# Sliding windows of an image batch: the last two units swapped, and the unit (14, 0) stored by GpSimd's indirect scatter in place of eight plain stores on SyncE's queue

## The chip, the cores and the metric

The kernel runs on one core of a Trainium2 chip. The metric is the device time of one execution in microseconds (us). The time of before is a median of 3 runs, and beside it stands one execution that the hardware profiler recorded. All times of single instructions come from that one execution.

## The reference: what is computed

The input `x` has 16 images of 64 channels, 64 rows and 64 columns in float32 (16.8 MB). The output holds every 8x8 window at a stride of 4. There are 15 window positions down (i) and 15 across (j), so 3600 windows of 64x8x8 elements, 59 MB. Nothing is calculated; bytes are copied from one layout to another.

```python
def reference(x, window_size, stride):
    n_h = (h - window_size) // stride + 1      # 15
    n_w = (w - window_size) // stride + 1      # 15
    result = np.zeros((batch, n_h, n_w, c, window_size, window_size), dtype=np.float32)
    for i in range(n_h):
        for j in range(n_w):
            result[:, i, j] = x[:, :, i*stride:i*stride+window_size, j*stride:j*stride+window_size]
    return result
```

One window of one image, `out[b, i, j]`, is 16 KB (64 channels x 64 floats x 4 bytes) and lies in one piece in device memory. "A row" below means these 16 KB.

## The kernel before, in words

**Input.** The whole input sits in one SBUF tile `L` (line 49). A partition holds 32 channels and 16 image rows of one image: partition number = 64 x channel half + 4 x image + image quarter (a quarter is 16 of the 64 rows). Loads (lines 103 to 107) go out on two queues: SyncE's (SP) takes 28 of the 32 channels of the first channel half, GpSimd's (POOL) the other four and all of the second half.

**Index tiles.** GpSimd makes a row of partition numbers (line 68), VectorE (DVE) computes from it the number of the output row that each partition writes (lines 79 to 101): `idx` for all rows, `idx_y0` and `idx_y1` for the images 0 to 7 or 8 to 15 alone, `idx_hi` and `idx_lo` for the lowest windows, where one of the 16 positions doesn't exist. A partition that has nothing to write gets an index beyond the bounds, and the scatter drops it.

**Units.** The output is made in units `(j, s)`: j is the window column, s is 0 or 2. A unit is one `G` tile of 128 partitions x 16 KB (line 112): one half of the partitions takes the windows that begin at slot s of each quarter (4 rows to a slot), the other half those of slot s + 1. There are four `G` tiles, used in turn. `fill` (lines 130 to 142) copies the windows out of `L`. For s = 0 ScalarE (ACT) does one copy of 64 partitions and DVE the other, for each half (line 172). For s = 2 (lines 182 to 184) ACT does both copies of slot 2, and DVE makes slot 3 with two copies and two shuffles, since slot 3 takes its lower four rows from the neighbouring partition. Which half takes slot 3 alternates with j (`turn`). Slot 3 of the last quarter doesn't exist, so such a unit writes 64 rows of slot 2 and 48 of slot 3, 112 rows; a unit with s = 0 writes 128.

**Stores.** `scatter` (lines 118 to 128) issues one indirect DMA on GpSimd's queue, which writes up to 128 rows of 16 KB. The stores are declared free of one another (lines 114 to 116), so no store waits for another one. A fill waits until the store that last read its `G` tile has landed, four units earlier.

**Order.** Six units over half of the images come first (lines 148 to 161), then the list `units` (line 164): for each j the unit (j, 0), if it wasn't among the first ones, and then (j, 2). Line 165 takes the second to last unit out of the list and puts it at its end, so that the last units are (13, 0), (13, 2), (14, 2), (14, 0). All units but the last go out by `scatter`. The last, (14, 0), goes out by eight plain DMAs on SP's queue (lines 176 to 179), one for each image quarter and slot, each of 16 rows, 256 KB. SP issues nothing else between the loads and these eight.

Of the kernel before, what the change touches and what calls it, by code (L numbers as in the profile page):

```python
# [10 lines left out]
def kernel(  # L11
# [7 lines left out]
    nc = tc.nc  # L19
# [11 lines left out]
    CH = 2  # L31
    HQ = P // (B * CH)
    CL = C // CH
    RB = H // HQ
    NSLOT = RB // ST
# [25 lines left out]
    def itile(name):  # L61
        return ipool.tile([P, 1], i32, name=name)

    pi, tb, tq, tc_, th, idx, idx_y0, idx_y1, idx_lo, idx_hi = (
        itile(n) for n in ("pi", "tb", "tq", "tc", "th", "idx", "idx_y0", "idx_y1", "idx_lo", "idx_hi")
    )
# [44 lines left out]
    NG = 4  # L111
    G = [gpool.tile([P, C, WS, WS], f32, name=f"G{n}") for n in range(NG)]

    def free(st):
        tc.declare_no_dep(st.ins, group="stores", reason="each store writes rows of its own")
        tc.add_to_no_dep_group("stores", st.ins)

    def scatter(g, ix, j, s):
        st = nc.gpsimd.indirect_dma_start(  # L119
            out=o_v,  # L120
            out_offset=bass.IndirectOffsetOnAxis(ap=ix[:, 0:1], axis=0),
            in_=g.rearrange("p c r w -> p (c r w)"),
            in_offset=None,
            element_offset=(s * NW + j) * CFREE,
            bounds_check=B * NWIN - 1,
            oob_is_err=False,
        )
        free(st)

    def fill(g, half, s, j, lo, n, copies):  # L130

        d = slice(half * HP + lo, half * HP + lo + n)
        cols = slice(j * ST, j * ST + WS)
        for ch in (half, 1 - half):
            f = slice(ch * HP + lo, ch * HP + lo + n)
            cs = slice(ch * CL, (ch + 1) * CL)
            copy = copies[ch != half]
            if s < NSLOT - 1:
                copy(out=g[d, cs, :, :], in_=L[f, :, s * ST : s * ST + WS, cols])  # L139
            else:  # L140
                copy(out=g[d, cs, 0:ST, :], in_=L[f, :, s * ST : RB, cols])  # L141
                nc.vector.stream_shuffle(out=g[d, cs, ST:WS, :], in_=L[f, :, 0:ST, cols], mask=nxt)  # L142
# [12 lines left out]
    for y in range(NY):  # L155
        for j in range(EARLY):
            for half in range(CH):
                copies = (dve, dve) if y and half and j == 1 else (act, dve)
                fill(G[t % NG], half, half, j, y * QP, QP, copies)
            scatter(G[t % NG], (idx_y0, idx_y1)[y], j, 0)  # L160
            t += 1


    units = [(j, s) for j in range(NW) for s in (0, 2) if s or j >= EARLY]
    units.append(units.pop(-2))
    o_q = out.rearrange("b i j c r w -> i j b (c r w)")
    for j, s in units:
        g = G[t % NG]
        t += 1
        if s == 0:  # L170
            for half in range(CH):
                fill(g, half, s + half, j, 0, HP, (act, dve))
            if (j, s) != units[-1]:
                scatter(g, idx, j, s)
                continue
            g_q = g.rearrange("(ch b q) c r w -> ch q b (c r w)", ch=CH, q=HQ)
            for q in range(HQ):
                for half in range(CH):
                    free(nc.sync.dma_start(out=o_q[q * NSLOT + s + half, j], in_=g_q[half, q]))
        else:  # L180

            turn = j % 2
            fill(g, turn, s, j, 0, HP, (act, act))
            fill(g, 1 - turn, s + 1, j, 0, HP, (dve, dve))
            scatter(g, (idx_hi, idx_lo)[turn], j, s)
# [35 lines left out]
```

## Time and profile before

| what | value |
|---|---|
| median of 3 runs (lowest to highest) | 196.81 us (196.72 to 196.84) |
| the profiled execution's own time | 196.84 us |
| its span, first to last instruction | 195.1 us |
| time of that execution outside the span | 1.74 us |
| DVE busy | 132.0 us (68%) |
| ACT busy | 123.6 us (63%) |
| POOL busy | 51.8 us (27%) |
| DMA, mean over the span | 75.81 MB at 389 GB/s |
| of it by GpSimd's queue (q0) | 66.34 MB, 83.3% of the span of 16 DMA engines |
| of it by SP's queue (q1) | 9.44 MB, 13.5% |
| indirect stores | 32, of 957 to 2194 ns on POOL; 5.9 to 20.5 us to landing |
| plain stores on SP | 8, 539 to 2418 ns each on SP's queue, from 175.0 us on |

Read it in this way. A busy share is a mean over stages that differ. DMA here means the 16 DMA engines that both queues share. "To landing" is the time from the issue of a DMA until its semaphore says that all bytes are written.

### The profile page before, as it was taken

The numbers are of one execution on the slowest core, as the hardware profiler recorded it, in microseconds if no ns is written. First come the engines' busy times: TensorE is split into PE (matmuls) and PEld (weight loads), VectorE is DVE, ScalarE is ACT, GpSimd is POOL, SyncE is SP. The second block draws the span as 40 slices with busy tenths as digits, with TensorE's granted clock in tenths as the row PEclk, the third lists the DMA queues.
The fourth block names the chain that finished last, engine by engine and source line by source line (L and its number), as shares of the span: only waits on it lengthen the run. The fifth ranks groups of instructions, "written<-read, shape, count | busy, mean of one in ns | idle before, by whom it ended". The sixth has DMA issues, their size and how long they took to land.

```text
span 195.1 us, 485 instructions
## 1 busy us (share of the span) xinstructions
DVE 132.0 (68%) x156; ACT 123.6 (63%) x66; POOL 51.8 (27%) x53
## 2 busy tenths in 40 slices
DVE  6877778895999998766577657774776667750000
ACT  0000008961999999999779677977797779752000
POOL 7402211107462134123313113231323132210000
DMA  2999999999999999999999999999999999999983
GB/s 87 316 403 403 398 402 394 403 399 408 420 375 380 386 420 403 427 420 415 430 430 415 417 417 420 423 423 420 430 423 420 420 427 410 410 418 420 329 259 124
DMA packets 11588, 75.81 MB, mean 389 GB/s; under 512 B 3888, under 2 KB 3888, under 8 KB 7984
## 3 DMA queue, kind: packets, MB, share of 16 engines
q0 software_dynamic: 9472, 66.34, 83.3%
q1 hardware_dynamic: 2112, 9.44, 13.5%
q14 instruction: 4, 0.03, 0.0%
HBM read 16.78 MB, written 69.21 MB: 441 GB/s over the span
## 4 chain that ended last, share of the span: by engine, by line
DMA 66%; DVE 17%; issue 3%; POOL 2%; ACTq 1%; ACT 1%; DVEq 0%; PEldq 0%
DMA out_dram<-G,idx 21%; DMA L<-in_x_dram 18%; DMA out_dram<-G,idx_hi 15%; DMA out_dram<-G,idx_lo 12%; DVE G L139 8%; DVE G L142 6%; DVE G L141 2%; POOL L L57 2%; ACTq L216 1%; ACT G L139 1%; DVEq L139 0%; POOL pi L68 0%; DVEq L141 0%; PEldq L216 0%; ACTq L139 0%
## 5 line engine op out<-in xcount | busy, mean ns | idle before, releaser
L139 ACT COPY G<-L 64x2048 f32<-64x2048 f32 (+1 forms) x65 | 122.3, 1896 | 23.5 <-DMA out_dram<-G,idx 9.9
L139 DVE COPY G<-L 64x2048 f32<-64x2048 f32 (+1 forms) x37 | 44.8, 1221 | 16.7 <-DMA out_dram<-G,idx 11.4
L142 DVE STREAM_SHUFFLE G<-L 64x1024 f32<-64x1024 f32 x30 | 38.3, 1276 | 0.0
L141 DVE COPY G<-L 64x1024 f32<-64x1024 f32 x30 | 20.7, 691 | 18.5 <-DMA out_dram<-G,idx_hi 10.4
L153 DVE MEMSET G<- 32x4096 f32 x8 | 27.8, 3472 | 7.9 <-issue 6.2
L139 ACT ACT_TABLE_LOAD x1 | 1.3, 1283 | 29.8 <-DMA L<-in_x_dram 29.8
L119 POOL DMA_INDIRECT out_dram<-G,idx_hi x8 | 11.7, 1461 | 30.3 <-DVE G L142 17.9
L119 POOL DMA_INDIRECT out_dram<-G,idx x11 | 11.4, 1040 | 30.6 <-ACT G L139 30.6
L57 POOL DMA_DIRECT2D L<-in_x_dram x16 | 9.8, 626 | 25.2 <-DMA L<-in_x_dram 24.7
L119 POOL DMA_INDIRECT out_dram<-G,idx_lo x7 | 9.1, 1304 | 20.5 <-ACT G L139 14.3
L119 POOL DMA_INDIRECT out_dram<-G,idx_y x6 | 9.4, 1559 | 13.4 <-DVE G L139 8.5
L77 DVE TENSOR_TENSOR th<-tc,tq 128x1 int32<-128x1 int32 x2 | 0.3, 160 | 0.1
L77 DVE CUSTOM_DVE_ANT_0 idx_y<-idx,th 128x2 uint16<-128x2 uint16 x2 | 0.3, 158 | 0.1
L74 DVE TENSOR_SCALAR th<-tc 128x1 int32<-128x1 int32 x2 | 0.3, 154 | 0.1
L68 POOL IOTA pi<- 128x1 int32 x1 | 0.1, 125 | 0.4 <-PEq L216 0.4
L77 DVE CUSTOM_DVE_ANT_0 idx_hi<-idx,th 128x2 uint16<-128x2 uint16 x1 | 0.2, 160 | 0.0
L142 DVE LOAD_MASK_SELECT G<-L x30 | 0.2, 6 | 0.0
L77 DVE CUSTOM_DVE_ANT_0 idx_lo<-tb,th 128x2 uint16<-128x2 uint16 x1 | 0.2, 159 | 0.0
L77 DVE CUSTOM_DVE_ANT_0 idx_lo<-idx_lo,th 128x2 uint16<-128x2 uint16 x1 | 0.2, 159 | 0.0
L77 DVE CUSTOM_DVE_ANT_0 idx<-tb,th 128x2 uint16<-128x2 uint16 x1 | 0.2, 159 | 0.0
L77 DVE CUSTOM_DVE_ANT_0 tb<-tb,th 128x2 uint16<-128x2 uint16 x1 | 0.2, 158 | 0.0
L91 DVE TENSOR_SCALAR th<-th 128x1 int32<-128x1 int32 x1 | 0.2, 153 | 0.0
(13 smaller groups left out, 1.7 us busy)
## 6 DMA issues: line engine op xcount, KB each, us to landing
L<-in_x_dram POOLq DMA_DIRECT2D x8, 1024.0 KB, 21.2
L<-in_x_dram SPq DMA_DIRECT2D x8, 896.0 KB
out_dram<-G SPq DMA_DIRECT2D x8, 256.0 KB
L<-in_x_dram POOLq DMA_DIRECT2D x8, 128.0 KB, 21.3
out_dram<-G,idx POOLq DMA_INDIRECT x11, 14.6
out_dram<-G,idx_hi POOLq DMA_INDIRECT x8, 13.9
out_dram<-G,idx_lo POOLq DMA_INDIRECT x7, 14.1
out_dram<-G,idx_y POOLq DMA_INDIRECT x6, 6.3
```

Of the source, the lines that this page charges most:

```text
L57: eng.dma_start(out=L[p0 : p0 + QP - HQ + 1 : HQ, c0:c1, :, :], in_=x_v[ch, y, q, :, c0:c1, :])
L68: nc.gpsimd.iota(pi[:, :], pattern=[[0, 1]], base=0, channel_multiplier=1)
L74: nc.vector.tensor_scalar(out=d[:, :], in0=a[:, :], scalar1=float(m), scalar2=None, op0=ALU.mult)
L77: nc.vector.tensor_tensor(out=d[:, :], in0=a[:, :], in1=b[:, :], op=op)
L91: nc.vector.tensor_scalar(out=th[:, :], in0=th[:, :], scalar1=-1.0, scalar2=FAR, op0=ALU.mult, op1=ALU.add)
L119: st = nc.gpsimd.indirect_dma_start(out=o_v, out_offset=bass.IndirectOffsetOnAxis(ap=ix[:, 0:1], axis=0), in_=g.rearrange("p c r w -> p (c ...
L139: copy(out=g[d, cs, :, :], in_=L[f, :, s * ST : s * ST + WS, cols])
L141: copy(out=g[d, cs, 0:ST, :], in_=L[f, :, s * ST : RB, cols])
L142: nc.vector.stream_shuffle(out=g[d, cs, ST:WS, :], in_=L[f, :, 0:ST, cols], mask=nxt)
L153: nc.vector.memset(G[t][p0 : p0 + QP, :, :, :], 0.0)
L216: with _tile.TileContext(nc) as tc:
```

## The change

Line 165 goes, so the last two units stand in the order (14, 0), (14, 2). The branch for the last unit goes too: (14, 0) is stored by `scatter` with `idx` like every other unit with s = 0, and (14, 2), now the last, by `scatter` with `idx_hi` as before. SP issues no stores any more. `free` is written out where it was called; that alters no instruction. Lines 67 to 107, which make the index tiles and issue the loads, and line 158, which hands copies to ACT or DVE, are the same in both kernels.

```diff
-    def free(st):
-        tc.declare_no_dep(st.ins, group="stores", reason="each store writes rows of its own")
-        tc.add_to_no_dep_group("stores", st.ins)
...
-        free(st)
+        tc.declare_no_dep(st.ins, group="stores", reason="each store writes rows of its own")
+        tc.add_to_no_dep_group("stores", st.ins)
...
     units = [(j, s) for j in range(NW) for s in (0, 2) if s or j >= EARLY]
-    units.append(units.pop(-2))
-    o_q = out.rearrange("b i j c r w -> i j b (c r w)")
     for j, s in units:
         g = G[t % NG]
         t += 1
         if s == 0:
             for half in range(CH):
                 fill(g, half, s + half, j, 0, HP, (act, dve))
-            if (j, s) != units[-1]:
-                scatter(g, idx, j, s)
-                continue
-            g_q = g.rearrange("(ch b q) c r w -> ch q b (c r w)", ch=CH, q=HQ)
-            for q in range(HQ):
-                for half in range(CH):
-                    free(nc.sync.dma_start(out=o_q[q * NSLOT + s + half, j], in_=g_q[half, q]))
+            scatter(g, idx, j, s)
         else:
             turn = j % 2
             fill(g, turn, s, j, 0, HP, (act, act))
             fill(g, 1 - turn, s + 1, j, 0, HP, (dve, dve))
             scatter(g, (idx_hi, idx_lo)[turn], j, s)
```

## The prediction

> **What bounds the kernel now.** I read the page's slices first, then the chain, then the tail in stretches, and then who ends last. The slices are 4.9 us wide; the first row is the share of the 16 DMA engines that is busy, the second what they move.
>
> ```profile
> DMA  2999999999999999999999999999999999999983
> GB/s 87 316 403 403 398 402 394 403 399 408 420 375 380 386 420 403 427 420 415 430 430 415 417 417 420 423 423 420 430 423 420 420 427 410 410 418 420 329 259 124
> ```
>
> From the third slice to the 37th the engines move some 400 to 430 GB/s: transfers bound the kernel. Then, in the last three slices, the rate falls to 329, 259 and 124. This is all that the change can touch, since the instructions ahead of the last two units are the same. The chain of work that ended last, from 140 us on, says what comes before that:
>
> ```profile
> 143.35 14.34 DMA out_dram<-G,idx
> 157.68 15.29 DMA out_dram<-G,idx_hi
> 172.98 0.02 issue
> ...
> 173.06 1.90 ACT G L139
> 174.96 1.92 ACTq L216
> ```
>
> The last fill begins when the store (12, 2) has landed, at 172.98, and frees its tile. From there the chain is cut off, so I looked at the tail by stretches of 2 us (stretch, DVE, ACT, POOL, clock, DMA share, GB/s).
>
> ```profile
> 172.00:174.00 2.00, 0.93 (x1) 0.94 (x1) 0.46 (x1) 1.00 1.06 442
> ...
> 182.00:184.00 2.00, 0.00 (x0) 0.00 (x0) 0.00 (x0) 1.00 0.99 336
> ...
> 186.00:188.00 2.00, 0.00 (x0) 0.00 (x0) 0.00 (x0) 1.00 0.80 246
> 188.00:190.00 2.00, 0.00 (x0) 0.00 (x0) 0.00 (x0) 1.00 0.79 262
> 190.00:192.00 2.00, 0.00 (x0) 0.00 (x0) 0.00 (x0) 1.00 0.84 238
> ```
>
> No engine computes after 177, yet the rate drops. The timeline and the rows of the last line that SP and POOL run (L216, the end of the program) name the two things that are late:
>
> ```profile
> 171.50 0.96 POOL L119 DMA_INDIRECT out_dram<-G,idx_hi  x1 [3.79 <-ACT G L139]
> 173.06 3.82 ACT L139 COPY G<-L 64x2048 f32<-64x2048 f32 x2 [2.35 <-DMA out_dram<-G,idx_hi]
> 173.07 2.48 DVE L139 COPY G<-L 64x2048 f32<-64x2048 f32 x2 [2.34 <-DMA out_dram<-G,idx_hi]
> 174.98 14.82 SPq L179 DMA_DIRECT2D out_dram<-G  x8
> ```
>
> ```profile
> L216 SPq EVENT_SEMAPHORE  x11: 17/28/28, 192.0 to 195.0; - x11
> L216 POOLq DRAIN  x3: 51/105/22757, 171.3 to 194.8; - x3
> ```
>
> First: SP needs 14.82 us to issue eight stores of 256 KB, until 189.8. Eight times 256 KB in 14.8 us is 142 GB/s, a third of what the engines can take, so once GpSimd's queue runs dry the engines starve. Second: POOL's first drain begins at 171.3 and takes 22.76 us, to 194.04. By the semaphore records of the trace the last scatter landed at 192.02 (issue 171.50 plus the longest time to landing, 20.5) and the last SP store at 194.14. SP's wait for it ends at 194.16, its own drain at 194.29, and the span ends 0.8 us later with the closing barrier.
>
> **The change part by part.** Sums are against the profiled execution: span 195.1, own time 196.84, so 1.74 us lie outside the span. The median of the runs shown is 196.81, so the two can be used as one.
>
> *Removed: eight plain stores.* 14.82 us on SP's queue go. Nothing was behind them but the end. What goes with them is the starved tail.
>
> *Moved: (14, 0) ahead of (14, 2).* The fill of (14, 0) takes the slot of (14, 2), at 166.88. ACT's two copies are the same (3.82 us, to 170.7), DVE's are shorter (2.48 against 3.83). So its scatter is issued at 171.5, where that of (14, 2) is now. The scatter adds one DMA_INDIRECT on POOL (0.96 to 1.78 us in the timeline after 60 us). POOL has its gap of 2 to 4 us before each scatter, so this costs nothing; the scatter behind it waits for copies until 177.7. Then (14, 2) is filled from 173.06, when (12, 2) has landed: ACT 3.82 us, DVE 3.83, both to 176.9. POOL starts 0.8 us later (170.7 to 171.50 in the row above), at 177.7, and is through by 179.5.
>
> *Is that early enough?* The price of a late scatter is a hole in the transfers. The first scatter of the kernel, issued at 44.53, has its first packets of over 8 KB in the stretch 46 to 48, so a scatter takes at most 3.5 us to its first rows: 181.2 at the latest here. By the semaphore records, the 16 increments of a scatter come in two bunches of eight: half of the engines run ahead. (13, 0) landed at 174.2 on the early half, at 176.8 on the late half, and on one engine at 177.6. A row of 16 KB takes 0.627 us on one engine (418 GB/s from 60 to 170 us, over 16). The early half has 16 rows to do for (13, 2) and (14, 0), so it is busy to 174.2 + 10.0 = 184.2. That leaves 3 us, so no hole.
>
> *When the last row lands.* Each engine has 22 rows left after (13, 0): a unit with s = 0 gives eight to every engine, one with s = 2 gives eight to one half and six to the other, and the halves swap from (13, 2) to (14, 2). 22 times 0.627 is 13.8 us. Early half: 188.0. Late half: 190.6. The one late engine: 191.4; it fell behind at 171.6, where the trace has a fetch of instructions of 8 KB, and that need not come at the same point again. I take 191.0, against 194.14 now: 3.1 us earlier.
>
> *What is late next.* Now GpSimd's drain stands behind the last landing, where today SP's stores cover it. It ended 2.0 us after the last scatter's landing (194.04 less 192.02). That a drain of 22.76 us waits for scatters, and isn't 22.76 us of work, is likely: the drains at the start and the end take 0.05 to 0.18 us. But no row shows what the 2.0 us consist of. The bounds for this lag are 0 (it may have been SP's own stores that kept it busy) and 22.8 (all of it work that begins only with the last scatter). I take 2.0, the one row there is.
>
> **Sum:** 191.0 + 2.0 + 0.8 (closing barrier) = 193.8 for the span, plus 1.74 = **195.5 us**, 0.7% less.
>
> [...] SP's first store was issued at 174.98. From 176 to 179.4 the trace has packets of q0 alone, 112 at a share of 1.01; the first of q1 come after that, 4.5 us after the issue. [...]
>
> **The rivals.**
>
> *No lag of the drain (faster still).* If the 2.0 us were SP's stores, or overlap, the end follows the last landing as it does now, 0.9 us later: 191.0 + 0.9 + 1.74 = 193.6; with the late half on time, 193.2. For it: the drain ended within 0.1 us of the last SP landing, which may be no accident. Against it: it is POOL's drain, and SP's stores aren't POOL's.
>
> *The drain lags more (slower).* Place: POOL's drain at L216, behind the scatter (14, 2), which is now issued at 177.7 and not 171.5. Today the eight plain stores hide what follows the last scatter; after the change nothing does. It decides from a lag of 196.81 - 1.74 - 0.8 - 191.0 = 3.3 us. At twice the lag, 4.0, the time is 197.5. At the bound, 22.8 us counted from the issue at 177.7, it is over 202. For it: 22.76 is by far the longest row of L216, and nothing but SP's stores hides it. Against: two out of those 22.76 us is all that lies behind a landing.
>
> *The gain is eaten up (no change).* A lag near 3.3 us, or a hole: if the first rows of (14, 2) came only 6.5 us after its issue, at 184.2, each further us would cost the early half first, which has 2.6 us in hand, so up to 9.1 us it would still cost nothing. So a hole needs a scatter nearly three times as slow as the first one; only the lag can do it.
>
> *The change doesn't do what it says.* Its few words speak of index tiles ahead of the loads and of evenly split copies. The diff touches neither; both kernels have them. If that was all that differed, nothing would change. What is in the diff is the order and the queue of the last two units, and I price that.
>
> **How the numbers follow.** Lag about 2.0 (195.0 to 196.2): 0.52, the forecast. No or little lag (193.2 to 195.0): 0.25. Lag near 3.3: 0.08. A larger lag: 0.15. Faster or slower by over 0.2% (0.4 us, about what a measurement of this kernel can tell from no change): the first two cases lie below 196.4, so faster 0.77; same 0.08; slower 0.15. The range leaves out the large lags and next to nothing below: 193.2 to 197.2.
>
> **What the profile after would show.** The rate at 400 GB/s and more until about 187, and no q1 packets after the loads. Scatter (14, 0) at 171.5 and (14, 2) at 177.7, or the fills were misjudged. The last landing at 190.6 to 191.4, or the count of rows is wrong. POOL's first drain ending some 2 us after that, and the span's end 0.8 us after the drain: this is the weakest step. If the span ends within 1 us of the last landing, the first rival holds; if the drain ends later than 194.3, the second.

## The result, and the profile after

The changed kernel takes 195.79 us (median of 4 runs, 195.64 to 195.95), the one before beside it 196.82 us (4 runs, 196.72 to 196.94). The ratio is 0.9947, with a 95% interval of 0.993 to 0.9965: 1.0 us faster. The profiled execution took 195.64 us with a span of 193.9, so 1.7 us lie outside the span again.

The slices of the page after, 4.85 us wide:

```profile
DMA  2999999999989999999999999999999999999980
GB/s 85 326 408 401 402 399 397 400 400 405 426 333 382 406 419 419 423 423 404 426 433 421 416 419 419 423 423 433 423 416 412 426 423 423 426 416 421 412 345 30
```

Where before had 329, 259 and 124 GB/s in its last three slices, the rate now holds for a slice longer (412), then comes 345, and 30 in the last slice, early in which the transfers end. The tail in stretches of 2 us (stretch, DVE, ACT, POOL, clock, DMA share, GB/s; these rows count a DMA packet wholly in the stretch in which it begins, so a share can be above 1):

```profile
180.00:182.00 2.00, 0.00 (x0) 0.00 (x0) 0.00 (x0) 1.00 1.00 426
...
184.00:186.00 2.00, 0.00 (x0) 0.00 (x0) 0.00 (x0) 1.00 0.97 410
186.00:188.00 2.00, 0.00 (x0) 0.00 (x0) 0.00 (x0) 1.00 0.79 336
188.00:190.00 2.00, 0.00 (x0) 0.00 (x0) 0.00 (x0) 1.00 0.42 180
190.00:192.00 2.00, 0.00 (x0) 0.00 (x0) 0.00 (x0) 1.00 0.00 0
```

At 190 to 192 before still moved 238 GB/s; here nothing moves after 190.6. But the span ends only at 193.9. The rows of the program's last line (L204 here) say why:

```profile
L204 SPq EVENT_SEMAPHORE  x11: 17/28/4457, 186.2 to 193.8; - x11
L204 POOLq DRAIN  x3: 51/105/16500, 176.6 to 193.6; - x3
```

The longest of SP's waits, 4457 ns from 186.59 on, is the one for the last scatter; it ends at 191.05 (the last landing is at 191.02). POOL's first drain begins at 176.57 and takes 16.50 us, to 193.07, which is 2.05 us after that landing. The last landing moved 3.1 us forward (194.14 to 191.02), the span's end 1.2 us. The rest of the gain went into the drain, which before lay beside SP's stores.

The last two scatters of the timeline after:

```profile
170.91 0.96 POOL L115 DMA_INDIRECT out_dram<-G,idx  x1 [2.73 <-ACT G L136]
...
176.79 0.96 POOL L115 DMA_INDIRECT out_dram<-G,idx_hi  x1 [4.92 <-issue]
```

### The profile page after: what moved, and what is told of

It reads as the page before. It is cut to its first block, busy times and chain, and to the rows that moved or that the text cites. A ratio compares the mean times of both kernels' runs of the same rounds, so it can differ in the third digit from the quotient of the medians.

```text
span 193.9 us, 478 instructions
## 1 busy us (share of the span) xinstructions
DVE 131.9 (68%) x156; ACT 123.5 (64%) x66; POOL 53.3 (27%) x54
## 4 chain that ended last, share of the span: by engine, by line
DMA 66%; DVE 17%; issue 6%; POOL 2%; POOLq 1%; DVEq 0%; PEldq 0%
DMA out_dram<-G,idx 21%; DMA L<-in_x_dram 18%; DMA out_dram<-G,idx_hi 14%; DMA out_dram<-G,idx_lo 12%; DVE G L136 8%; DVE G L139 6%; DVE G L138 3%; POOL L L57 2%; POOLq L204 1%; DVEq L136 0%; POOL pi L68 0%; DVEq L138 0%; PEldq L204 0%
## 5 line engine op out<-in xcount | busy, mean ns | idle before, releaser
L115 POOL DMA_INDIRECT out_dram<-G,idx x12 | 12.4, 1030 | 33.3 <-ACT G L136 33.3
L115 POOL DMA_INDIRECT out_dram<-G,idx_lo x7 | 9.7, 1390 | 20.5 <-ACT G L136 14.3
```

Source lines behind the costliest of these rows:

```text
L115: st = nc.gpsimd.indirect_dma_start(out=o_v, out_offset=bass.IndirectOffsetOnAxis(ap=ix[:, 0:1], axis=0), in_=g.rearrange("p c r w -> p (c ...
```

## The experiments

"Landing" below is the last semaphore increment of a store in the trace, and the end of the drain is its start plus its duration. Edits are to the kernel before, unless the text says otherwise.

### The order of the last two units

The changed kernel with line 165 put back: both units by scatter, (14, 0) last.

```diff
     units = [(j, s) for j in range(NW) for s in (0, 2) if s or j >= EARLY]
+    units.append(units.pop(-2))
```

> The changed kernel with the old order of the last two units: (14, 2), then (14, 0), both by GpSimd's scatter. Theory (the end is the last landing, which 22 rows per engine after (13, 0) set, plus POOL's drain 2.0 us after it): each engine has the same rows, so the last landing stays at 190.3 to 191.1, the drain ends 2.0 us later, and the time is that of the changed kernel, 195.8, within 0.4. Rival (the order of the two units is what gains): 196.5 to 197.

195.40 us against 196.78; ratio 0.9934 (0.9921 to 0.9948), an interval that overlaps that of the changed kernel. The last landing was at 190.72, the drain ended at 192.77. So the order gains nothing; dropping the plain stores does it all.

### The plain stores earlier

```diff
-    units.append(units.pop(-2))
...
-            if (j, s) != units[-1]:
+            if (j, s) != units[-2]:
```

> The kernel before with line 165 out: (14, 0) by SP's eight plain stores, then (14, 2) last by GpSimd's scatter. Theory (the plain stores cost only where their slow issue, 14.8 us for eight, ends after everything else): they are issued from 171 to 186, some 4 us earlier than before, the engines stay full, the last scatter lands near 191 and the drain follows 2.0 us later: 195.5 to 196.0. Rival (plain stores beside scatters slow the engines by themselves): 196.5 or more, with a rate under 400 GB/s before 186.

198.80 us; ratio 1.0111 (1.0096 to 1.0127), slower than before. The first row is SP's issue in the timeline, the others are stretches of the tail:

```profile
168.62 14.49 SPq L178 DMA_DIRECT2D out_dram<-G  x8
```

```profile
174.00:176.00 2.00, 1.91 (x3) 1.50 (x1) 0.00 (x0) 1.00 0.81 328
...
186.00:188.00 2.00, 0.00 (x0) 0.00 (x0) 0.00 (x0) 1.00 0.98 320
```

The issue ended at 183.1, 11 us before the last landing (194.15), and scatters were in the queue throughout. Yet the rate is 337 GB/s from 178 to 188 at a DMA share of 0.99. The engines aren't starved; they are slow while these plain stores run beside scatters. The last landing is as late as in before (194.14). The time is 2.0 us longer because this landing is now a scatter's: GpSimd's drain ends 2.0 us behind it, at 196.15, where in before it lay beside SP's stores. My theory of the tail, a slow issue, fell here, and the rival held.

### The plain stores from two queues

```diff
-                    free(nc.sync.dma_start(out=o_q[q * NSLOT + s + half, j], in_=g_q[half, q]))
+                    free((nc.sync, nc.scalar)[half].dma_start(out=o_q[q * NSLOT + s + half, j], in_=g_q[half, q]))
```

> The kernel before, but its eight plain stores alternate between SP's and ACT's queue. Theory (the tail of before starves on the issue by one queue): issue takes about half, 7.4 us, and ends near 183; the rate holds near 400 GB/s to 187 and all lands by 191. The drain then ends 2.0 us after the last scatter, between 191 and 193: 194.2 to 195.7. Rival (the DMA engines, not the issue, are slow with two kinds of stores in the tail): 196.5 to 197.

198.38 us; ratio 1.0085 (1.0071 to 1.0099). The timeline has the issues, the stretch the rate that followed:

```profile
174.83 5.30 SPq L179 DMA_DIRECT2D out_dram<-G  x4
176.76 6.30 ACTq L179 DMA_DIRECT2D out_dram<-G  x4
```

```profile
178.00:188.00 10.00, 0.00 (x0) 0.00 (x0) 0.00 (x0) 1.00 1.01 341
```

All was issued by 183.1 in place of 189.8, and the last landing came at 193.56, only 0.6 us earlier than in before. That the time still grew, beyond both ranges that were expected, is the drain again: the last landing is a scatter's (the last plain store landed at 193.46), and GpSimd's drain ended behind it, at 195.57.

### What the drain waits for

The changed kernel, with loads that nothing uses behind all stores.

```diff
             scatter(g, (idx_hi, idx_lo)[turn], j, s)
+
+    for y in range(NY):
+        for q in range(HQ):
+            load(nc.sync, 0, y, q, SMALL, CL)
```

> The changed kernel with extra work: SP loads its 28 channels of the input once more into L after all fills (8 loads, 7.3 MB), which nothing uses. The loads reach only some of the engines, so they land long after the last scatter. Theory (POOL's drain waits for GpSimd's own DMAs alone): it ends 2.0 us after the last scatter's landing and many us before the span's end, and the span ends 0.9 us after the last load. Rival (the drain waits for all DMAs of the core): it ends 2 us after the last load, the span 2.8 us after it.

One run, 229.17 us, and the rows of its last line:

```profile
L208 POOLq DRAIN  x3: 51/105/19810, 176.6 to 227.1; - x3
L208 SPq DRAIN  x3: 7/7/7, 226.5 to 226.9; - x3
```

The last scatter landed at 194.37 and the drain ended at 176.61 + 19.81 = 196.42, 2.05 us later and 30 us before the last load (226.47). The span ended 0.9 us after that load. So the drain waits for GpSimd's own DMAs, not for all of them. It lags by 2.0 us whatever else goes on (in the runs below that the table leaves out and that end GpSimd's DMAs with a scatter, 2.01 to 2.05):

| kernel | last scatter lands | drain ends | lag | last plain DMA lands |
|---|---|---|---|---|
| before | 192.02 | 194.04 | 2.02 | 194.14 |
| after | 191.02 | 193.07 | 2.05 | none |
| old order, both scattered | 190.72 | 192.77 | 2.05 | none |
| plain stores earlier | 194.15 | 196.15 | 2.00 | 191.38 |
| plain stores from two queues | 193.56 | 195.57 | 2.01 | 193.46 |
| late loads | 194.37 | 196.42 | 2.05 | 226.47 |
| eight DMAs across the halves (below) | 189.00 | 191.01 | 2.01 | 190.64 |

### What slows the engines: the queue, the rows written or the partitions read

A plain store of before reads 16 partitions four apart, all in one half of the tile, and its 16 rows go to 16 engines (16 landings in its semaphore records). In before, the packets of these rows took 0.89 us in the mean and up to 1.50 (packet records of the trace), where a scatter's row takes 0.62 in the changed kernel. From 178 to 188 before moved this:

```profile
178.00:188.00 10.00, 0.00 (x0) 0.00 (x0) 0.00 (x0) 1.00 0.99 329
```

Three kernels part the causes.

One queue for all: the eight plain stores are issued by GpSimd.

```diff
-                    free(nc.sync.dma_start(out=o_q[q * NSLOT + s + half, j], in_=g_q[half, q]))
+                    free(nc.gpsimd.dma_start(out=o_q[q * NSLOT + s + half, j], in_=g_q[half, q]))
```

> The kernel before with the eight plain stores issued on GpSimd's queue in place of SP's: same bytes, same partitions, one queue. What is open: with plain stores beside scatters the rate was 320 to 340 GB/s, even where the issue was early. [...] Theory B (two queues on each engine disturb one another): one queue, so 400 GB/s and more, all landed by 191: 195.4 to 196.2.

199.06 us, just above the 197.5 to 199 that I had estimated for a rate that stays near 330 GB/s (337 and 341 in the two runs above), with the drain 2.0 us behind the last landing; ratio 1.0121 (1.0102 to 1.0139).

```profile
182.00:184.00 2.00, 0.00 (x0) 0.00 (x0) 0.00 (x0) 1.00 1.00 238
184.00:186.00 2.00, 0.00 (x0) 0.00 (x0) 0.00 (x0) 1.00 1.02 287
```

With a single queue the rate is as bad, and packets after 182 took up to 1.50 us. The time itself says less, since GpSimd issued the last store only at 188.8, after a wait of 7.0 us for an earlier DMA. The drain behind it ended at 196.53, 2.3 us after the last landing (194.19), somewhat more than behind a scatter.

One whole DMA: SP writes the tile's 128 partitions in order to a scratch tensor, and the unit's output rows are left out.

```diff
-            g_q = g.rearrange("(ch b q) c r w -> ch q b (c r w)", ch=CH, q=HQ)
-            for q in range(HQ):
-                for half in range(CH):
-                    free(nc.sync.dma_start(out=o_q[q * NSLOT + s + half, j], in_=g_q[half, q]))
+            o_s = nc.dram_tensor("scratch", (P, CFREE), f32).ap()
+            free(nc.sync.dma_start(out=o_s, in_=g.rearrange("p c r w -> p (c r w)")))
```

> The kernel before, but the unit (14, 0) isn't stored to its output rows: SP writes the whole tile, 128 partitions in order, 2.1 MB, by one plain DMA to a scratch tensor in device memory. [...] Theory B (two queues): 320 to 340 GB/s, 196.5 to 198.8.

195.40 us; ratio 0.9929 (0.9912 to 0.9947). The queues from 176 to 186 us:

```profile
DMA packets 320, 4.19 MB, mean 419 GB/s; under 512 B 64, under 2 KB 64, under 8 KB 64
...
q0 software_dynamic: 240, 2.88, 68.2%
q1 hardware_dynamic: 80, 1.31, 30.8%
```

Two queues at work on the same engines move 419 GB/s (426 from 180 to 186; q1's first row begins at 181.18), and no packet of q1 took over 0.622 us. So the two queues don't disturb one another here.

Eight DMAs with the partitions of before, written to consecutive rows of a scratch tensor:

```diff
+            o_s = nc.dram_tensor("scratch", (P, CFREE), f32).ap()
...
-                    free(nc.sync.dma_start(out=o_q[q * NSLOT + s + half, j], in_=g_q[half, q]))
+                    r0 = (2 * q + half) * B
+                    free(nc.sync.dma_start(out=o_s[r0 : r0 + B], in_=g_q[half, q]))
```

> The kernel before, but the eight plain stores of (14, 0) read the same partitions (16, four apart) and write to consecutive rows of a scratch tensor, not to their output rows, which lie 3.7 MB apart. Theory A (pattern of partitions read): nothing changes, 196.4 to 197.2. Theory C (rows far apart in device memory): as fast as one whole DMA, under 195.8. Theory B (two queues) expects 196.4 to 197.2 as well; the run with the whole tile tells A from B.

196.72 us; ratio 1.0005 (0.9993 to 1.0016): as before.

```profile
178.00:188.00 10.00, 0.00 (x0) 0.00 (x0) 0.00 (x0) 1.00 1.01 356
```

So it isn't where the rows lie in device memory that costs the time. Whether it has a small part in the rate is open: in this trace the plain stores' rows took 0.79 us in the mean and the rate was 356 GB/s, against 0.89 and 329 in before. And the whole DMA differs from the eight in their number too, so two more kernels kept the eight, and the scratch rows, and changed the partitions alone.

### Eight DMAs, other partitions

```diff
-            g_q = g.rearrange("(ch b q) c r w -> ch q b (c r w)", ch=CH, q=HQ)
...
-                    free(nc.sync.dma_start(out=o_q[q * NSLOT + s + half, j], in_=g_q[half, q]))
+            g_p = g.rearrange("p c r w -> p (c r w)")
+            o_s = nc.dram_tensor("scratch", (P, CFREE), f32).ap()
+            for n in range(8):
+                free(nc.sync.dma_start(out=o_s[n * B : (n + 1) * B], in_=g_p[QP + n % HQ : QP + n % HQ + B * HQ - HQ + 1 : HQ]))
```

> The kernel before; the unit (14, 0) isn't stored to its output rows. SP issues eight plain DMAs of 16 rows as before, to consecutive rows of a scratch tensor, but each reads partitions 32 + q, 36 + q, up to 92 + q, so half of its rows from either half of the tile (64 of the 128 rows, each twice). It differs from the run with 16 rows of one half in the partitions read alone, and from the run with one whole DMA in the number of DMAs. [...] Rival (eight small DMAs and their slow issue cost by themselves): 196.4 or more, as with the other eight.

193.74 us; ratio 0.9841 (0.9824 to 0.9857). SP's issues, the stretch of 178 to 188, and the drain:

```profile
L179 SPq DMA_DIRECT2D scratch<-G x8: 555/1372/1384, 175.6 to 184.6; - x8
```

```profile
178.00:188.00 10.00, 0.00 (x0) 0.00 (x0) 0.00 (x0) 1.00 0.94 398
```

```profile
L216 POOLq DRAIN  x3: 51/105/19656, 171.4 to 191.5; - x3
```

The same number of DMAs of the same size on the same queue, to the same scratch rows; only the partitions differ, and the rate is full. No row of the plain stores took over 0.633 us. One issue takes 1372 ns in the median where before has 1886: part of the "slow issue" came from the slow transfers. The time went below the 195.2 to 195.8 that I had estimated for a full rate with the last landing by 191.2, because the plain stores now land late enough after the last scatter to hide the drain, and at full rate: the last scatter has landed at 189.00, and its drain (191.01) lies beside the last plain landing (190.64).

The other one reads neighbouring partitions; of its edit only the last line is shown, which takes the place of the last line above:

```diff
+                free(nc.sync.dma_start(out=o_s[n * B : (n + 1) * B], in_=g_p[n * B : (n + 1) * B]))
```

> As the last one, but each of the eight DMAs reads 16 neighbouring partitions (0 to 15, 16 to 31 and so on), all 128 rows once. [...] Rival (number and issue of the DMAs): 196.4 to 197.

201.34 us; ratio 1.0209 (1.0177 to 1.0241).

```profile
L179 SPq DMA_DIRECT2D scratch<-G x8: 358/2324/3658, 174.9 to 189.6; - x8
```

```profile
178.00:180.00 2.00, 0.00 (x0) 0.00 (x0) 0.00 (x0) 1.00 1.87 352
180.00:182.00 2.00, 0.00 (x0) 0.00 (x0) 0.00 (x0) 1.00 0.16 49
...
178.00:188.00 10.00, 0.00 (x0) 0.00 (x0) 0.00 (x0) 1.00 1.01 239
```

Rows of the plain stores took 1.41 us in the mean and up to 4.4 in the profiled execution, the slowest of the four (202.52 us). The shares of 1.87 and 0.16 are to be read together: long packets that begin in the one stretch run on into the other, and over both the share is 1.0. Over the ten microseconds it is 1.01, at 239 GB/s: the engines are busy, and each row takes longer.

The three runs with eight DMAs to scratch rows differ in the partitions read alone. Rows of 0.79, 0.615 and 1.41 us and times of 196.72, 193.74 and 201.34 us go with them. So it is shown that the partitions from which the 16 rows of a DMA are read set the rate here. The queue doesn't (329 GB/s from 178 to 188 us in before, 323 with the eight on GpSimd's queue), nor does the number of DMAs (411 with the one whole DMA, 398 with eight across the halves). Why some sets of partitions are slower to read than others, no run shows.

### A version that beats both: the halves balanced

The changed kernel with the old order of the last two units, and the other half first to take slot 3.

```diff
+    units.append(units.pop(-2))
...
-            turn = j % 2
+            turn = 1 - j % 2
```

> Both last units scattered, in the order (14, 2), (14, 0), and turn = 1 - j % 2, so that the half of the partitions that writes six rows per engine and not eight is the other one in every unit with s = 2. Theory (the late half of the engines has 8 x 2 rows less to skip than the early one, and ends 2.6 us later): eight units now spare the late half and seven the early one, so its lead changes by 4 rows, 2.5 us; both halves end near 189, 1.3 us earlier, and the time is 194.0 to 194.6. Rival (the halves are not what sets the end; the one late engine is): 195.2 to 195.8.

194.46 us (194.37 to 194.77); ratio 0.9889 (0.9873 to 0.9904). All output rows are written.

```profile
186.00:188.00 2.00, 0.00 (x0) 0.00 (x0) 0.00 (x0) 1.00 0.94 401
188.00:190.00 2.00, 0.00 (x0) 0.00 (x0) 0.00 (x0) 1.00 0.16 66
```

```profile
L205 POOLq DRAIN  x3: 51/105/17203, 174.6 to 192.3; - x3
```

With the old order and `turn` as it was, the last scatter landed at 187.4 to 187.6 on the early half of the engines and at 189.9 to 190.7 on the late one. Here it is 188.2 to 188.5 and 188.9 to 189.8. Each unit with s = 2 spares one half two rows per engine, and with 15 such units one half is spared once more; it now is the half that was late.

## Why the prediction was right, and where its reason was wrong

**The sum held, term by term.** Last landing: 191.0 forecast, 191.02 measured; late half 190.6 against 190.1 to 190.3, late engine 191.4 against 191.02. Lag of the drain: 2.0 against 2.05. Closing barrier: 0.8 against 0.8 (193.07 to the span's end). Span: 193.8 against 193.9; time: 195.5 against 195.64 in the profiled execution and 195.79 in the median, so 1.0 us gained where 1.3 was forecast. That the landing fits to 0.02 us is luck: 191.0 was picked between 190.6 and 191.4, and the late engine was less late than in before. The lag was one row taken over without knowing what it consists of; it held.

**"SP needs 14.82 us to issue eight stores ... once GpSimd's queue runs dry the engines starve" was wrong.** It was the step that was to explain the falling rate. In the tail of before, scatters and plain stores stood in the queues together and the engines were busy (share 1.01) at 325 GB/s from 180 to 186. Two runs whose issue ended 6.7 us earlier, at 183.1, had their last landing at 194.15 and 193.56, where before has 194.14; so the faster issue was worth 0.6 us at most. With partitions across both halves the last landing came at 190.64, although the issue ended only at 186.0. What costs the rate is the reading of 16 rows from one half. Some idle time is there too: from 186 to 192 the share in before is 0.79 to 0.84, and no run tells how much of that is the issue. The sum came out right nonetheless, since it only needed that the rate is full without these stores. I had the sign to hand and passed over it: the DMA share stayed at 0.99 at 182 to 184 us while the rate was 336. Starved engines would have shown a lower share.

**Copies and scatters.** Forecast: scatters at 171.5 and 177.7, measured 170.91 and 176.79, 0.6 and 0.9 us earlier. The store (12, 2) landed at 171.73 and not at 172.98, and the fetch of instructions behind which one engine was late in before came at 177.2 in place of 171.6. As forecast, this cost no hole: the rate is 405 GB/s from 178 to 188.

**No lag of the drain** (the first rival, 0.25): fell. SP issues no stores and the lag is still 2.05 us; with 30 us of loads behind it, it doesn't follow them. That the drain of before ended within 0.1 us of the last SP landing was an accident. **A larger lag**, and one near 3.3 us that eats the gain (the rivals on the slower side): fell, the lag is 2.00 to 2.05 us in every row of the table. **Nothing changes, since only what the words say differs:** fell, the scatters and stores changed as the diff says.

**The start of the last unit's store** didn't set the end. In the changed kernel the engines had rows to move (422 GB/s from 176 to 178, 405 from 178 to 188) when the last unit was issued, at 176.79. The whole DMA of 2.1 MB, issued at 176.97 behind full queues, had its first row at 181.18, 4.2 us later. At the start of before, with nothing queued, SP's first load had its first packet at 2.35, 1.6 us after its issue began and 0.7 us after it ended.

**Two readings of the prediction are off**, and nothing rests on them: slices 12 to 14 of before have 375 to 386 GB/s, not 400 to 430, and the longest DMA_INDIRECT after 60 us takes 1.83 us, not 1.78.

## What to carry to other kernels

When the rate falls in a tail, look at the DMA share beside it, over several microseconds. Where the share was low here (0.42 at 180 GB/s from 188 to 190 us in the changed kernel, when one half of the engines was through), engines were without work, and in such a place the issue may be late. Where it was full at a low rate (0.99 at 329 GB/s from 178 to 188 us in before, 1.01 at 239 with neighbouring partitions), rows took longer (0.89 and 1.41 us in the mean against 0.62), and the cause lay in the partitions that each DMA reads, not in the queue. The kernels here that end GpSimd's DMAs with a scatter paid a drain of 2.00 to 2.05 us behind it. Plain stores lay beside that drain where the last of them landed 2.12 us (before) or 1.64 us (eight across the halves) after the last scatter, and they were as fast per row as the scatters they replace only in the second (0.615 us against 0.62). The whole-tile DMA was as fast, but landed beside the last scatter (191.16 and 190.98), and the drain still ended the kernel at 192.99. Count the rows per engine over the whole kernel: a remainder of one unit on one half of the engines was worth 0.9 us here (195.40 to 194.46).

## What the runs showed of the hardware that was not expected

- Sixteen rows of 16 KB, read from one half of the partitions in steps of four, take 0.89 us a row in the mean in the tail of before, and 0.79 us when they are written to scratch rows; read across both halves in the same steps and written to scratch rows, 0.615 us; from 16 neighbouring partitions, 1.41 us.
- The scatters beside them are slowed too: from 178 us on, a scatter's row took up to 1.33 us in before and up to 1.57 with neighbouring partitions, against 0.625 at most across both halves. In the stretch of 178 to 188 us all queues together moved 329, 239 and 398 GB/s.
- Issuing one plain DMA of 16 rows on SP's queue took 1.37 us in the median where the transfers ran at full rate, 1.89 in before and 2.32 with neighbouring partitions.
- GpSimd's drain ends 2.00 to 2.05 us after the last scatter's landing in the eleven kernels whose last DMA of GpSimd's is a scatter, and 2.3 us after the landing where it is a plain store.

Left open: what the drain does in its 2.0 us. Not tried: a last unit that is laid out so that real output rows can be stored from partitions across both halves, with the drain beside it, as the scratch version had it at 193.74 us.
